# Attention block: the fourth head's scores behind six more value products, and an early load of the exponential's table

## The chip, the cores and the metric

The kernel runs on one core of a Trainium2 chip. The metric is the device time of one execution in microseconds (us). The kernel before takes 1063.34 us, the median of 3 runs (1062.45 to 1063.61).

The core's engines each work through an instruction list of their own, in order, and wait for one another through semaphores: TensorE (PE in the profile, with its weight loads as PEld), VectorE (DVE), ScalarE (ACT), GpSimd (POOL), and SyncE (SP), which here only starts DMA transfers.

## The reference, cut to what matters

The model has two layers. Each layer is a gated feed-forward block, a mixer (convolution, gated recurrence, pooling), cross attention to a memory of 256 rows, and a second feed-forward block, each followed by a layer norm. There are 256 tokens and the model width is 1024. The change is in the cross attention alone:

```python
def cross_attn(x, mem, wq, wk, wv, wo):
    bsz, s, _ = x.shape
    m = mem.shape[1]
    q = (x @ wq).reshape(bsz, s, CA_HEADS, CA_HEAD_DIM)
    k = (mem @ wk).reshape(bsz, m, CA_HEADS, CA_HEAD_DIM)
    v = (mem @ wv).reshape(bsz, m, CA_HEADS, CA_HEAD_DIM)
    sc = jnp.einsum('bshd,bmhd->bhsm', q, k).astype(jnp.float32) * (CA_HEAD_DIM ** -0.5)
    p = jax.nn.softmax(sc, axis=-1).astype(v.dtype)
    o = jnp.einsum('bhsm,bmhd->bshd', p, v).reshape(bsz, s, D_MODEL)
    return o @ wo
```

There are 4 heads of width 256. Everything is computed in float32.

## The kernel before, in words

Every matrix product is made of three products of halves. A float32 operand x is split into a high part (x rounded, one ScalarE copy, line 75) and a low part (x minus the high part, one VectorE subtraction, line 76), and a product is high x high, high x low and low x high, added up in PSUM. The helper `split` issues both steps, and the helper `product` (line 132) issues every one of these matrix products, so that most rows of TensorE have line 132 and most rows of ScalarE and VectorE have lines 75 and 76. Rows are told apart by their tiles.

A weight matrix comes in pieces of 512 KB into tiles named `raw` (6 buffers); ScalarE makes `whi` from each and VectorE `wlo` (8 buffers each). All loads of weights are started by SP.

The attention of one layer goes as follows. Heads are numbered from 0.

1. `values(l, 0, ...)`: values of heads 0 and 1 (columns 0 to 511), before the stretch that matters.
2. `query(0)`: the first 512 columns of the queries (heads 0 and 1), in two passes `p` of two column blocks each. A pass ends with `split(qTh, qTl, o)`: the queries' high part on ScalarE and their low part on VectorE.
3. `query(1, ...)`: the second 512 columns (heads 2 and 3). Between its two passes `weights(0)`, `deal(0)`, `weights(1)`, `deal(1)` are issued. Its first pass ends in the queries of head 2, its second in those of head 3.
4. `values(l, 1, ...)`: values of heads 2 and 3. Its loop runs over two blocks `i` of memory rows and 8 blocks `k` of the contraction, with three products for each; a dictionary says what is issued in front of a pair of blocks. Key 2 is i = 0, k = 4; key 3 is i = 0, k = 6; keys 6 and 7 are i = 1, k = 4 and k = 6. Before, key 2 holds `weights(2)`, `weights(3)`, then `turned(0)`, `turned(1)`, `deal(2)`, `deal(3)`.
5. `project_back`: the output projection, whose slabs of two contraction blocks need `xT`, the attention's output; between the first slab and the rest it issues `others`, that is `turned(2)`, `turned(3)`, `mixed(2)` and `mixed(3)`.

`weights(hh)` is a head's 12 score products into a PSUM tile `dn`, a row maximum (line 1372) and its scaling (line 1373) on VectorE, two exponentials on ScalarE (line 1379, tile `e`), and the reciprocal and scaling on VectorE (lines 1384 and 1387). `deal(hh)` is four transfers of 64 KB from `e` to `dealt`, started by SP (line 1395). `turned(hh)` transposes blocks on VectorE (line 1404) and splits the result into `pTh` and `pTl`, or, for heads 2 and 3, into the places of `qTh` and `qTl`. `mixed(hh)` is 12 products of those with the values and the split of their sums into `xTh` and `xTl`.

ScalarE reads its functions from a table. The compiler puts an ACT_TABLE_LOAD in front of an activation whose function is not in the table that is loaded; in the attention this is the exponential of head 0.

The order on each engine is set when the program is built, by a scheduler that follows the order in which the code issues instructions and lets an engine take a later instruction first where its own estimate has it ready earlier. `tc.issue_after(x)` ties an instruction behind x on x's engine.

Of the kernel before, what the change touches and what calls it, by code (L numbers as in the profile page):

```python
# [8 lines left out]
F32 = mybir.dt.float32  # L9
F32R = mybir.dt.float32r  # L10
U8 = mybir.dt.uint8
AF = mybir.ActivationFunctionType
# [5 lines left out]
P = 128  # L18
# [42 lines left out]
def model(ctx: ExitStack, tc: tile.TileContext, t: dict, out: bass.AP):  # L61
    nc = tc.nc
    cst = ctx.enter_context(tc.tile_pool(name="cst", bufs=1))
    wp = ctx.enter_context(tc.tile_pool(name="wp", bufs=1))
    sm = ctx.enter_context(tc.tile_pool(name="sm", bufs=2))
    ps = ctx.enter_context(tc.tile_pool(name="ps", bufs=4, space=PSUM))

    def acc(shape=(P, 2, SEQ), tag="acc"):
        return ps.tile(list(shape), F32, tag=tag, name=tag)
# [4 lines left out]
    def split(hi, lo, src):  # L74
        rounded = nc.scalar.copy(hi, src)  # L75
        lows.append(nc.vector.tensor_tensor(lo, src, hi.bitcast(F32), op=ALU.subtract))  # L76
        return rounded
# [63 lines left out]
    def mm_cols(w, cols, x):  # L141
        o = acc()
        for k in range(NK - 1):
            product(o, w.at(k, cols)[0], x[:, k], k == 0, False)
        for k in range(NK):
            product(o[:, 0, :], w.at(k, cols)[1], x[:, k, 0, :], False, False)
        product(o, w.at(NK - 1, cols)[0], x[:, NK - 1], False, True)
        return sums(o)

    def add(dst, o):  # L150
        dst = dst if len(dst.shape) == 3 else halves(dst)
        nc.scalar.copy(dst, o[:, 1])
        nc.vector.tensor_tensor(dst, o[:, 0], dst, op=ALU.add)  # L153


    def mm_rows(o, xh, xl, wh, wl, start, stop, more=False):
        product(o, xh, wh, start, False, more)
        product(o, xh, wl, False, False, more)
        product(o, xl, wh, False, stop, more)

    def tok(i):
        return slice(i * P, (i + 1) * P)
# [7 lines left out]
    nhalf = cst.tile([P, 16], F32, name="nhalf")[:, 0:HEADS]  # L170
# [151 lines left out]
    def ln_params(l, n):  # L322
        g = wp.tile([P, DM], F32, tag="lng", name="lng")
        b = wp.tile([P, DM], F32, tag="lnb", name="lnb")
        nc.sync.dma_start(g, t["ln_g"][l, n : n + 1, :].to_broadcast([P, DM]))
        nc.sync.dma_start(b, t["ln_b"][l, n : n + 1, :].to_broadcast([P, DM]))
        return g, b
# [645 lines left out]
    def values(l, c, vh, vl, between={}, held=None):  # L973
        w = load(t["ca_v"][l], 0, NK, c * CHUNK, CHUNK, across=True)
        for i in range(NT):
            o = acc((P, 512))
            for k in range(NK):
                if k % 2 == 0:
                    between.get(4 * i + k // 2, lambda: None)()
                wh, wl = w.at(k, slice(0, CHUNK))  # L980
                mm_rows(o, mT[:, k, 0, tok(i)], mT[:, k, 1, tok(i)], wh, wl, k == 0, k == NK - 1)
            d = slice(c * CHUNK, (c + 1) * CHUNK)
            part = (halves(vh[:, i, d]), halves(vl[:, i, d]), sums(o))
            if held is None or i:
                split(*part)
            else:
                nc.scalar.copy(part[0], part[2])
                held.append(part)
# [352 lines left out]
    def attention(l, pend):  # L1341
        scale = (DM // HEADS) ** -0.5
        with tc.tile_pool(name="att", bufs=1, reuse_waits="tile") as ap:
            qTh = ap.tile([P, NK, SEQ], F32R, name="qTh")
            qTl = ap.tile([P, NK, SEQ], F32R, name="qTl")
# [4 lines left out]
            def query(c, between=None):  # L1350

                with tc.issue_after(normed[-1].ins):
                    w = load(t["ca_q"][l], 0, NK, c * CHUNK, CHUNK, across=True)
                for p in range(2):
                    o = sm.tile([P, 2, SEQ], F32, tag="sums", name="sums", bufs=1)
                    for j in range(2):
                        add(o[:, j, :], mm_cols(w, slice((2 * p + j) * P, (2 * p + j + 1) * P), xT))
                    d = slice(4 * c + 2 * p, 4 * c + 2 * p + 2)
                    split(qTh[:, d, :], qTl[:, d, :], o)
                    if between is not None and p == 0:  # L1360
                        between()

            def weights(hh):
                o = acc(tag="dn")
                for i in range(NT):
                    for d in (2 * hh, 2 * hh + 1):
                        mm_rows(
                            o[:, i, :], qTh[:, d, tok(i)], qTl[:, d, tok(i)], kTh[:, d, :], kTl[:, d, :],
                            d == 2 * hh, d != 2 * hh,
                        )  # L1370
                mx = sm.tile([P, NT], F32, tag="mx", name="mx")
                nc.vector.tensor_reduce(mx, o, axis=AX.X, op=ALU.max)
                nc.vector.tensor_scalar_mul(mx, mx, -scale)


                e = ap.tile([P, NT * SEQ], F32, tag="e", name="e", bufs=2)
                s = sm.tile([P, NT], F32, tag="sum", name="sum")
                for i in range(NT):
                    nc.scalar.activation(  # L1379
                        e.rearrange("p (a m i j) -> p i m a j", m=2, i=2, j=32)[:, i],  # L1380
                        o[:, i, :].rearrange("p (a j h) -> p h a j", h=2, j=32),
                        AF.Exp, bias=mx[:, i : i + 1], scale=scale, accum_out=s[:, i : i + 1],
                    )
                nc.vector.reciprocal(s, s)
                for i in range(NT):
                    v = e.rearrange("p (q i j) -> p i q j", i=2, j=32)[:, i]
                    nc.vector.tensor_scalar_mul(v, v, s[:, i : i + 1])
                es[hh] = e


            def deal(hh):
                e = es[hh]
                x = ap.tile([P, 4, 4, 32], F32, tag="dealt", name="dealt", bufs=2)
                for a in range(4):
                    nc.sync.dma_start(x[a * 32 : a * 32 + 32], e[:, a * P : (a + 1) * P])
                pr[hh] = x

            def turned(hh):

                if hh < 3:  # L1400
                    pt = sm.tile([P, 2, SEQ], F32, tag="sums", name="square", bufs=1)
                else:
                    pt = ap.tile([P, NT * SEQ], F32, tag="e", name="e", bufs=2).rearrange("p (m t) -> p m t", m=2)
                nc.vector.transpose(pt.rearrange("p m (i b r) -> p b (m i) r", i=2, b=4), pr[hh])
                if hh < 2:
                    pTh = ap.tile([P, NT, SEQ], F32R, tag="pTh", name="pTh", bufs=2)
                    pTl = ap.tile([P, NT, SEQ], F32R, tag="pTl", name="pTl", bufs=2)
                else:

                    pTh, pTl = (x[:, 2 * hh - 4 : 2 * hh - 2, :] for x in (qTh, qTl))  # L1410
                split(pTh, pTl, pt)
                return pTh, pTl
# [19 lines left out]
            pT = []  # L1432
            held = []

            def turned_rows():
                pend()
                hi, lo, o = held.pop()
                with tc.issue_after(lows[-1].ins):
                    lows.append(nc.vector.tensor_tensor(lo, o, hi.bitcast(F32), op=ALU.subtract))

            values(l, 0, vh, vl, {6: turned_rows}, held)
            query(0)
            gb = ln_params(l, 2)
            query(1, lambda: (weights(0), deal(0), weights(1), deal(1)))
            values(
                l, 1, vh, vl,
                {
                    2: lambda: (weights(2), weights(3), pT.extend((turned(0), turned(1))), deal(2), deal(3)),

                    6: lambda: mixed(0, pT[0]),  # L1450
                    7: lambda: mixed(1, pT[1]),
# [18 lines left out]
    for l in range(DEPTH):  # L1470
        started, pend = ffn(
            l, "ffn1", 0, pend, early=None if l else beginnings, started=started,
            following=(lambda: key_weights(l, 0, True)) if l else None,
        )
        keys(l, 0, {6: pend}, started)
        pend = mixer(l, lambda: keys(l, 1))
        pend = attention(l, pend)
        end = l == DEPTH - 1
        started, pend = ffn(
            l, "ffn2", 3, pend, last=end,  # L1480
            following=None if end else lambda: load(t["ffn1_gate"][l + 1], 0, NK, 0, CHUNK, hold=True),
        )
# [27 lines left out]
```

## Time and profile before

| | |
|---|---|
| median of 3 runs | 1063.34 us |
| the profiled execution's own time | 1062.75 us |
| its span, first to last instruction | 1061.0 us |
| TensorE busy | 1050.8 us, 99% of the span |
| VectorE busy | 921.5 us, 87% |
| ScalarE busy | 667.4 us, 63% |
| mean granted TensorE clock | 0.998 |
| TensorE's share of the chain that ended last | 96% |

The profile is of one execution. Times in the prediction are microseconds from the start of its span. A row of the timeline has a start, a duration, the engine, the line, the operation, the tiles (out <- in), the shape, and how many equal instructions it merges; in brackets stands the engine's idle time ahead of it and what ended it. Matmuls overlap, so a row's duration is longer than the step from its start to the next start; the step is what a product costs. The chain that ended last is followed back from the last instruction: at each step to what released it, or to the instruction ahead of it on its engine.

The attention's stretch that the change touches lies at 313 to 348 us in layer 0 and at 836 to 871 us in layer 1.

### The profile page before, as it was taken

Reading aid. Unit: us, or ns where it says so; the run is one execution under the profiler, and the core shown is the slowest. Engines: PE = TensorE matmul, PEld = TensorE weight load, DVE = VectorE, ACT = ScalarE, POOL = GpSimd, SP = SyncE. Lnnn points to the kernel's source line nnn. Section 1 sums busy time; section 2 is a strip of 40 time slices with the busy share of each in tenths; the row PEclk is TensorE's granted clock in tenths of the full one; section 3 lists DMA queues with packets and bytes.
Section 4 is the critical chain, followed back from the end, with each engine's and each line's share of the span. In section 5 each row is a group of like instructions: output and inputs, shape, how many; then the busy total and the mean of one; then the engine's idle time right before and its main releaser. Section 6 shows DMA issues by size and latency. Waiting matters only on the chain.

```text
span 1061.0 us, 16440 instructions
## 1 busy us (share of the span) xinstructions
PE 1050.8 (99%) x5998; PEld 933.0 (88%) x5998; DVE 921.5 (87%) x1228; ACT 667.4 (63%) x917; POOL 99.6 (9%) x137
## 2 busy tenths in 40 slices
PE   9999999999999999999999999999999999999997
PEld 7888888889898888888888888998998998888896
DVE  6998898989898789887898887899898888888787
ACT  6675775676657567655665656666775655675661
POOL 8002001000100001010001001010001000000001
PEclk9999999999999999999999999999999999999999
DMA  9999984854775589978789988876637775799972
GB/s 362 297 300 298 260 276 145 268 166 155 231 252 197 168 281 233 365 187 229 230 302 258 339 220 217 269 229 222 204 119 231 250 235 169 244 297 297 236 199 69
DMA packets 142689, 252.11 MB, mean 238 GB/s; under 512 B 11376, under 2 KB 52112, under 8 KB 142608
## 3 DMA queue, kind: packets, MB, share of 16 engines
q1 hardware_dynamic: 130656, 228.89, 65.2%
q0 software_dynamic: 11376, 20.99, 11.4%
q10 hardware_dynamic: 576, 1.18, 0.3%
q8 instruction: 47, 0.77, 0.3%
q14 instruction: 34, 0.28, 0.1%
HBM read 234.50 MB, written 1.05 MB: 222 GB/s over the span
## 4 chain that ended last, share of the span: by engine, by line
PE 96%; DVE 2%; ACT 1%; DMA 1%; issue 0%; DVEq 0%; ACTq 0%; SPq 0%
PE acc L132 62%; PE dn L132 30%; DVE wlo L76 1%; PE acc L203 1%; PE dn L1174 0%; DMA raw<-in_ca_v_dram 0%; ACT whi L75 0%; PE dn L1248 0%; DMA h<-in_x_dram 0%; ACT e L1379 0%; DVE qTl L76 0%; PE acc L615 0%; PE dn L1247 0%; PE dn L1236 0%; DVE sums L153 0%
## 5 line engine op out<-in xcount | busy, mean ns | idle before, releaser
L76 DVE TENSOR_TENSOR wlo<-raw,whi 128x1024 fp32r<-128x1024 f32 (+1 forms) x452 | 533.5, 1211 | 58.5 <-ACT whi L75 51.9
L75 ACT CAST whi<-raw 128x1024 fp32r<-128x1024 f32 (+1 forms) x452 | 456.4, 1041 | 184.9 <-PE acc L132 48.7
L132 PE MATMUL acc<-whi,xT 128*128 128x512 f32 (+1 forms) x1064 | 313.9, 372 | 0.0
L132 PEld LDWEIGHTS acc<-whi,xT 128*128 128x128 f32 x1064 | 199.1, 189 | 26.9 <-DVE halves L755 0.3
L132 PE MATMUL acc<-wlo,xT 128*128 128x512 f32 (+1 forms) x532 | 197.9, 372 | 0.0
L132 PE MATMUL dn<-whi,ah 128*128 128x512 f32 x346 | 131.5, 380 | 0.0
L132 PE MATMUL dn<-wlo,ah 128*128 128x512 f32 x346 | 131.2, 379 | 0.0
L132 PE MATMUL dn<-whi,al 128*128 128x512 f32 x346 | 131.1, 379 | 0.0
L132 PE MATMUL acc<-xT,whi 128*128 128x512 f32 x480 | 118.6, 381 | 0.0
L132 PEld LDWEIGHTS acc<-wlo,xT 128*128 128x128 f32 x532 | 100.6, 189 | 13.4
L132 PEld LDWEIGHTS acc<-xT,whi 128*128 128x128 f32 x480 | 86.5, 190 | 9.5
L132 PE MATMUL dn<-whi,xT 128*128 128x512 f32 x288 | 87.4, 380 | 0.0
L132 PEld LDWEIGHTS dn<-whi,al 128*128 128x128 f32 x346 | 65.4, 189 | 9.2
L132 PEld LDWEIGHTS dn<-wlo,ah 128*128 128x128 f32 x346 | 65.4, 189 | 9.2 <-DVE wlo L76 0.3
L132 PEld LDWEIGHTS dn<-whi,ah 128*128 128x128 f32 x346 | 65.4, 189 | 8.9
L132 PEld LDWEIGHTS acc<-xT,wlo 128*128 128x128 f32 x480 | 63.8, 191 | 3.8
L132 PE MATMUL acc<-xT,wlo 128*128 128x256 f32 x480 | 64.5, 275 | 0.0
L132 PE MATMUL acc<-whi,kTh 128*128 128x512 f32 (+1 forms) x176 | 62.0, 352 | 0.0
L132 PE MATMUL acc<-wlo,kTh 128*128 128x512 f32 (+1 forms) x176 | 61.7, 351 | 0.0
L132 PE MATMUL acc<-whi,kTl 128*128 128x512 f32 (+1 forms) x176 | 61.7, 351 | 0.0
L132 PEld LDWEIGHTS dn<-whi,xT 128*128 128x128 f32 x288 | 54.4, 189 | 7.7 <-DVE xT L76 0.3
L132 PE MATMUL dn<-wlo,xT 128*128 128x512 f32 x144 | 54.6, 379 | 0.0
(261 smaller groups left out, 1287.6 us busy)
## 6 DMA issues: line engine op xcount, KB each, us to landing
raw<-in_ffn_up_dram SPq DMA_DIRECT2D x88, 512.0 KB, 5.8
raw<-in_ffn_down_dram SPq DMA_DIRECT2D x88, 512.0 KB, 6.0
raw<-in_ffn_gate_dram SPq DMA_DIRECT2D x84, 512.0 KB, 5.5
raw<-in_w_in_dram SPq DMA_DIRECT2D x48, 512.0 KB, 4.7
dealt<-sg SPq DMA_DIRECT2D x80, 128.0 KB, 4.8
raw<-in_ffn_up_dram POOLq DMA_DIRECT2D x19, 512.0 KB, 6.3
raw<-in_ffn_gate_dram POOLq DMA_DIRECT2D x16, 512.0 KB, 9.2
raw<-in_ca_k_dram SPq DMA_DIRECT2D x16, 512.0 KB, 5.0
```

The source lines that it names most:

```text
L75: rounded = nc.scalar.copy(hi, src)
L76: lows.append(nc.vector.tensor_tensor(lo, src, hi.bitcast(F32), op=ALU.subtract))
L132: turns.append(nc.tensor.matmul(o, w, x, start=start, stop=stop, skip_group_check=more))
L203: turns.append(nc.tensor.transpose(pt[:, k - 4 * j, :], of_k, unit))
```

## The change

Two things are changed, both in the attention of each layer.

- `weights(3)` and `deal(3)` are moved from key 2 to key 3 of `values(l, 1, ...)`: the six products of k = 4 and 5 now stand between the scores of head 2 and those of head 3, and `turned(0)`, `turned(1)` and `deal(2)` are issued ahead of head 3.
- Behind the last high part of `query(0)` ScalarE gets one activation of 128x1 elements, the exponential of a constant, into a tile `ready` that nothing reads. The tile takes a turn in the two buffers named `rs`. The table load is therefore placed there, and no longer in front of head 0's exponential.

```diff
                     d = slice(4 * c + 2 * p, 4 * c + 2 * p + 2)
-                    split(qTh[:, d, :], qTl[:, d, :], o)
+                    rounded = split(qTh[:, d, :], qTl[:, d, :], o)
                     if between is not None and p == 0:
                         between()
+                return rounded
...
             values(l, 0, vh, vl, {6: turned_rows}, held)
-            query(0)
+            rounded = query(0)
+            with tc.issue_after(rounded.ins):
+                nc.scalar.activation(sm.tile([P, 1], F32, tag="rs", name="ready"), nhalf[:, 0:1], AF.Exp)
             gb = ln_params(l, 2)
             query(1, lambda: (weights(0), deal(0), weights(1), deal(1)))
             values(
                 l, 1, vh, vl,
                 {
-                    2: lambda: (weights(2), weights(3), pT.extend((turned(0), turned(1))), deal(2), deal(3)),
+                    2: lambda: (weights(2), pT.extend((turned(0), turned(1))), deal(2)),
+                    3: lambda: (weights(3), deal(3)),
```

The built programs differ in the attention of the two layers and nowhere else, in the same way in both. Lines behind the added ones are one to four higher in the changed kernel.

On TensorE, where the scores of heads 2 and 3 stand in the middle of the value products (`dn` is a head's scores, `acc` the sum of the values):

```order
 L132 MATMUL dn<-kTl,qTh 128x256
 L132 MATMUL dn<-kTh,qTl 128x256
+L132 MATMUL acc<-whi,mT_1456 128x512
+L132 MATMUL acc<-wlo,mT_1456 128x512
+L132 MATMUL acc<-whi,mT_1456 128x512 x2
+L132 MATMUL acc<-wlo,mT_1456 128x512
+L132 MATMUL acc<-whi,mT_1456 128x512
 L132 MATMUL dn<-kTh,qTh 128x256
 L132 MATMUL dn<-kTl,qTh 128x256
```

Six value products moved from behind head 3's scores to a place between head 2's and head 3's.

On ScalarE, from the end of the first query chunk to where head 0's exponential follows:

```order
 L75 CAST whi<-raw 128x1024
 L75 CAST qTh<-sums 128x512
+L1445 ACT_TABLE_LOAD
+L1445 ACTIVATE ready<-nhalf 128x1
 L152 COPY sums<-acc 128x256 x2
 L75 CAST qTh<-sums 128x512
-L1379 ACT_TABLE_LOAD
```

The table load moved ahead of three copies and casts of the second chunk's first pass, with the small activation behind it.

On VectorE, behind the value products of i = 0, from the low parts of two weight pieces (`wlo`) on; `xT` is the attention's output, the transpose is head 2's; first as it was:

```order
L76 TENSOR_TENSOR wlo<-raw,whi 128x1024 x2
L76 TENSOR_TENSOR xT<-acc,xT 128x256
L1404 STREAM_TRANSPOSE square<-dealt 128x4x4x32
L76 TENSOR_TENSOR xT<-acc,xT 128x256
L76 TENSOR_TENSOR wlo<-raw,whi 128x1024
L76 TENSOR_TENSOR xT<-acc,xT 128x256
```

and as it is now:

```order
L76 TENSOR_TENSOR wlo<-raw,whi 128x1024 x2
L76 TENSOR_TENSOR xT<-acc,xT 128x256
L1405 STREAM_TRANSPOSE square<-dealt 128x4x4x32
L76 TENSOR_TENSOR wlo<-raw,whi 128x1024
L76 TENSOR_TENSOR xT<-acc,xT 128x256 x2
L76 TENSOR_TENSOR qTl<-square,qTh 128x512
```

The low part of one weight piece moved ahead of the second low part of head 0's output (`xT`).

On SP, the transfers behind the dealing of heads 0 and 1 (`raw` from `ca_o` are pieces of the output projection, from `ffn_gate` and `ffn_up` of the next block's weights):

```order
 L103 DMA raw<-in_ca_o_dram 128x1024 x2
-L103 DMA raw<-in_ffn_gate_dram 128x2x512
-L1395 DMA dealt<-e 32x4x128 x8
-L103 DMA raw<-in_ffn_gate_dram 128x2x512 x3
+L103 DMA raw<-in_ffn_gate_dram 128x2x512 x2
+L1396 DMA dealt<-e 32x4x128 x8
+L103 DMA raw<-in_ffn_gate_dram 128x2x512 x2
 L103 DMA raw<-in_ffn_up_dram 128x2x512 x4
```

A second piece of the next block's gate weights moved ahead of the eight transfers that deal heads 2 and 3.

## The prediction

> **What bounds the kernel now.** I read the page first, then who waited for whom on TensorE, then the chain that ended last through the attention, and last the timelines of the engines in it.
>
> ```profile
> span 1061.0 us, 16440 instructions
> PE 1050.8 (99%) x5998; PEld 933.0 (88%) x5998; DVE 921.5 (87%) x1228; ACT 667.4 (63%) x917; POOL 99.6 (9%) x137
> PE dn L596 <- DVE kTh L591: 1.5, 1, 1.5
> PE dn L132 <- DVE qTl L76: 0.6, 2, 0.4
> PE acc L615 <- DMA h<-in_x_dram: 0.4, 1, 0.4
> ```
>
> TensorE is the bound. Its waits are three rows. The first and third are the program's start; the middle one, twice, is for `qTl`, the low part of the queries. So an edit in the attention can win what hangs on that row, or nothing. The chain through layer 0's attention shows where it comes from:
>
> ```profile
> 315.51 2.68 PE dn L132 x24
> 318.19 2.64 PE acc L132 x16
> ...
> 321.84 0.66 ACT e L1379 x3
> ...
> 327.49 0.70 DVE qTl L76
> ...
> 328.23 1.38 PE dn L132 x10
> 329.61 10.45 PE acc L132 x60
> ```
>
> From 320.83 to 328.23 the chain leaves TensorE: over exponentials and what stands behind them to `qTl` of head 3, for which head 3's scores wait. Then TensorE again. The starts of the products tell what the wait costs (heads 0 and 1 first, then layer 0's heads 2 and 3, then layer 1's):
>
> ```profile
> 315.35 0.27 PE L132 MATMUL dn<-kTh,qTh 128*128 128x256 f32 x1
> 318.03 1.68 PE L132 MATMUL acc<-xT,whi 128*128 128x512 f32 x7
> ...
> 323.27 0.38 PE L132 MATMUL acc<-whi,mT 128*128 128x512 f32 x1
> 325.86 0.27 PE L132 MATMUL dn<-kTh,qTh 128*128 128x256 f32 x1
> 327.38 0.38 PE L132 MATMUL dn<-kTh,qTh 128*128 128x256 f32 x1
> 328.23 0.38 PE L132 MATMUL dn<-kTh,qTl 128*128 128x256 f32 x1 [0.35 <-DVE qTl L76]
> 329.44 0.38 PE L132 MATMUL acc<-whi,mT 128*128 128x512 f32 x1
> ...
> 849.14 0.27 PE L132 MATMUL dn<-kTh,qTh 128*128 128x256 f32 x1
> 851.07 0.38 PE L132 MATMUL dn<-kTh,qTl 128*128 128x256 f32 x1 [0.20 <-DVE qTl L76]
> 852.28 0.38 PE L132 MATMUL acc<-whi,mT 128*128 128x512 f32 x1
> ```
>
> Heads 0 and 1 put 24 score products into 318.03 - 315.35 = 2.68 us, 0.112 each, with no wait. The same 24 for heads 2 and 3 take 329.44 - 325.86 = 3.58 us in layer 0 and 852.28 - 849.14 = 3.14 us in layer 1. The stall is 0.90 + 0.46 = **1.36 us**, more than the bracketed idle time, since the starts behind a wait are also spread.
>
> **The change part by part.**
>
> *Six products ahead of head 3.* Nothing is added. Twelve value products take 325.86 - 323.27 = 2.59 us, so six take 1.30. Head 2 starts at 325.86 as before and its 12 products end at 327.20; the six end at 328.50; head 3's third product, the first to read `qTl`, comes two steps later, at 328.72. `qTl` was there at 327.49 + 0.70 = 328.19, so this edit alone covers it, by 0.5 us. In layer 1 the need moves to 849.14 + 1.34 + 1.30 + 0.22 = 852.00, and 851.07, when the waiting product started, bounds the readiness: 0.9 us. The high part is cast ahead of the low part and is covered with it.
>
> *The table load in front of the second chunk.*
>
> ```profile
> 313.19 0.61 ACT L75 CAST qTh<-sums 128x512 fp32r<-128x512 f32 x1
> 315.75 0.65 ACT L152 COPY sums<-acc 128x256 f32<-128x256 f32 x2 [1.94 <-DVE qTl L76]
> ...
> 319.27 1.28 ACT L1379 ACT_TABLE_LOAD   x1 [1.16 <-DVE mx L1373]
> 320.56 0.47 ACT L1379 ACTIVATE e<-dn,mx 128x256 f32<-128x256 f32 x1
> 320.94 0.19 ACT L1379 ACTIVATION_READ_ACCUMULATOR e<-dn,mx 128x1 f32 x1
> ...
> 838.86 0.65 ACT L152 COPY sums<-acc 128x256 f32<-128x256 f32 x2 [1.95 <-PE acc L132]
> 842.11 1.28 ACT L1379 ACT_TABLE_LOAD   x1 [0.88 <-DVE mx L1373]
> ```
>
> The load, 1.28 us, leaves the path of the exponentials and lands in a gap of 1.94 us (1.95 in layer 1) between a cast and the copies. With it goes one activation of 128x1, which the trace does not have. From below it is bounded by the 128x1 read of the accumulator, 0.19, from above by an exponential over 256 columns, 0.47; I take 0.2, as its size is that of the first. So 1.47 to 1.75 us in a gap of 1.94: cost nothing, hidden by ScalarE's wait for the copies' inputs. Without that cover, each 0.1 us over delays the copies, whose queries head 2 reads at 325.86, ten microseconds later: still nothing on TensorE, only less of the gain for the exponentials. The gain is up to 1.28 us on all that stands behind them on ScalarE: copy, casts, `qTh` of head 3, and so `qTl`, to 328.19 - 1.28 = 326.9. That alone would meet the old need at 327.20 + 0.22 = 327.42. Both edits remove the same stall, each alone; they do not add. The second one adds margin, not time.
>
> *What is late next.* TensorE comes 0.90 us earlier to all that follows, and head 3's scores end at 328.50 + 1.34 = 329.84 against 329.44, 0.40 us later. The rows that carry what follows:
>
> ```profile
> 333.51 0.62 DVE L1387 TENSOR_SCALAR e<-e,sum 128x256 f32<-128x256 f32 x2
> 335.25 2.35 DVE L76 TENSOR_TENSOR wlo<-raw,whi 128x1024 fp32r<-128x1024 f32 x2
> 337.85 0.71 DVE L1404 STREAM_TRANSPOSE square<-dealt 128x512 f32<-128x512 f32 x1
> 338.47 0.39 DVE L76 TENSOR_TENSOR xT<-acc,xT 128x256 fp32r<-128x256 f32 x1
> 339.32 1.23 DVE L76 TENSOR_TENSOR wlo<-raw,whi 128x1024 fp32r<-128x1024 f32 x1 [0.46 <-ACT whi L75]
> 341.62 0.59 PE L132 MATMUL dn<-whi,xT 128*128 128x512 f32 x2
> 344.05 0.68 DVE L76 TENSOR_TENSOR qTl<-e,qTh 128x512 fp32r<-128x512 f32 x1
> 346.42 0.28 PE L132 MATMUL acc<-qTh,vh 128*128 128x256 f32 x1
> ```
>
> Head 3's scaling ended at 334.13; I put it at 334.5 to 334.7. The two low parts behind it started at 335.25 because `pTl` and `vl` stood between; in the new order these come earlier, so the pair starts at about 334.7, 0.55 earlier. The second `xT` low part ended at 338.86. Now one low part of a weight (1.23) is ahead of it: 338.86 - 0.55 + 1.23 = 339.5. The first slab's product that reads it started at 341.62 and would now at 340.72. The slack falls from 2.8 to **1.2 us**, and stays positive. For head 3's `qTl<-e`, 344.73 before, the same items stand ahead in another order; I put it between 344.1 and 344.7. Its reader, one step after 346.42 - 0.90, comes at 345.6: about 0.9 to 1.5 us. Nothing is lost.
>
> *The transfers.*
>
> ```profile
> 333.47 5.08 SPq L1395 DMA_DIRECT2D dealt<-e  x8
> dealt<-e SPq DMA_DIRECT2D x32, 64.0 KB, 2.1
> dealt<-both SPq DMA_DIRECT2D x6, 64.0 KB, 4.8
> raw<-in_ffn_gate_dram SPq DMA_DIRECT2D x84, 512.0 KB, 5.5
> ```
>
> A second gate piece of 512 KB now starts ahead of the dealing of heads 2 and 3. It needs a `raw` buffer that VectorE frees with the weight's low part behind `qTl` (328.19 + 1.23 = 329.4 before, up to 1.28 earlier now), so it does not hold SP, which has nothing else to start until head 2 is scaled. Head 2's scaling should end near 332.7 and its four transfers, 0.63 us apart, start by 334.6 and land 2.1 us later, 336.7, ahead of the transposition, wanted at 337.85 - 0.55 = 337.3. The gate piece, at 5.5 us, started near 328.2, lands at 333.7, before most of them start. I take 2.1.
>
> The Trainium skill (DMA: Bandwidth & Descriptors, "Queues, rings and completion order") says that on each DMA engine the descriptors of one issuing queue are consumed in ring order, so that the dealing would wait for what is left of the gate piece. The two rows of `dealt` spread from 2.1 to 4.8, which fits, but nothing here shows that the ring is why. By that rule the sum would lose up to what the second rival below gives; by the row of 2.1 it loses nothing.
>
> **The sum.** The profiled execution took 1062.75 us, 1.75 around its span of 1061.0. Less 1.36 that is 1061.39. The median of the runs stands 0.59 above the profiled time: 1061.39 + 0.59 = **1062.0 us**, 0.13% faster. That is inside the 0.2% (2.1 us) that a measurement of this kernel can tell from no change.
>
> **The rivals.**
>
> *First: ScalarE's path is the bound, and the whole table load is won.* The chain passes through the exponentials in both layers, which speaks for it: 2 x 1.28 = 2.57 us, 1062.75 - 2.57 + 0.59 = 1060.8 us. Against it, the three rows of waits: TensorE waits for nothing else there, and work that comes earlier than TensorE needs it is worth nothing.
>
> *Second, slower: the dealing lands late behind the added gate piece.* The transposition then stands at the head of VectorE's queue, and the weight's low part and the second `xT` low part wait behind it. At 4.8 us, as for `dealt<-both`, head 2's last transfer lands at 339.4, 2.1 after it is wanted; past the slack of 1.2 that is 0.9 us in each layer: 1.8 - 1.36 = +0.4, or 1063.8 us. It costs from a landing time of 3.9 us on, and turns the sign at 4.6; at 5.5, as for the gate pieces themselves, it would be 1.6 per layer, 3.2 - 1.36 = +1.8, and 1065.2 us. Against it, the gate piece should have landed before. The rule of ring order raises its chance from 2 to 5 in 100.
>
> *Third: the wait moves and the time stays.* The first slab (slack 1.2) or head 3's mixing (0.9 to 1.5) waits instead, because my placing of VectorE's work may be a microsecond off. The price is at most what was won: 1062.75 to 1061.39, plus 0.59, so 1062.0 to 1063.3; I call it 1063.0.
>
> *Fourth: the change does not do what it says.* The built order has both moves, and the load waits for nothing ahead of it; only the small activation could hold ScalarE. At 0.47 it still fits. I give it 1 in 100, at 1063.3.
>
> **How the numbers follow.** Forecast 0.75, first rival 0.09, second 0.05, third 0.10, fourth 0.01. The three runs lie 0.89 below to 0.27 above their median. The range goes from the first rival's 1060.8, with a little of that spread, to the third's 1063.3 and the second's 1063.8: **1060.6 to 1063.8 us**. Faster by over 0.2% (below 1061.2): the first rival and about a tenth of the forecast's runs, 0.16. Slower by over 0.2% (above 1065.5): the second rival beyond a landing of 5.7 us and stray runs, 0.04. Within: 0.80.
>
> **What would show it.** TensorE's waits should lose the `qTl` row in both layers. From head 2's first product to the next value product behind head 3 there should be 2.68 + 1.30 = 3.98 us. ScalarE should show a load of 1.28 and an activation of about 0.2 behind `qTh`, with the copies starting at the same distance from it as before, and the first exponential right behind `mx`, about 1.3 us earlier. Transfers of `dealt` should land in 2.1 us. The forecast is wrong if the span shrinks by more than 2 us (first rival), if VectorE idles ahead of its transposition of `dealt` (second), or if TensorE gets a row of waits for `xT` or for the transposed weights (third).

## The result, and the profile after

The changed kernel takes 1061.46 us, the median of 22 executions, against 1063.55 us for the kernel before in 22 executions on the same chip: a ratio of 0.9981, 95% interval 0.9975 to 0.9987, so 2.0 us less (the medians themselves differ by 2.1). The forecast was 1062.0 us, 1.36 us less. With all later executions pooled (44 of the changed kernel, 155 of the kernel before, on several chips) the means differ by 2.0 us, with an interval of 1.7 to 2.3 from resampling them. So the direction was forecast and the size was too small; most of what follows is about that difference.

The page of the changed kernel, and its table of what TensorE waited for:

```profile
span 1061.0 us, 16436 instructions
PE 1050.1 (99%) x5998; PEld 932.8 (88%) x5998; DVE 920.5 (87%) x1228; ACT 668.8 (63%) x919; POOL 99.8 (9%) x137
PE dn L596 <- DVE kTh L591: 1.5, 1, 1.5
PE acc L132 <- DVE halves L755: 1.5, 2, 1.3
PE acc L615 <- DMA h<-in_x_dram: 0.4, 1, 0.4
```

The row for `qTl` is gone. The span is no shorter than that of before, because this one execution (1062.78 us, 1.3 above the median) has two waits, 1.5 us together, for `halves` in the feed-forward blocks (1.3 of it in layer 1's second one), which the profile of before does not have. One profile against one profile would have read as no change; the attention has to be looked at by itself. The timeline of TensorE there, layer 0, heads 2 and 3:

```profile
326.31 0.27 PE L132 MATMUL dn<-kTh,qTh 128*128 128x256 f32 x1
...
328.94 0.27 PE L132 MATMUL dn<-kTh,qTh 128*128 128x256 f32 x1
...
329.17 0.28 PE L132 MATMUL dn<-kTh,qTl 128*128 128x256 f32 x1
...
330.28 0.38 PE L132 MATMUL acc<-whi,mT 128*128 128x512 f32 x1
```

From head 2's first product to the value product behind head 3 it takes 330.28 - 326.31 = 3.97 us (forecast 3.98): 24 score products, six value products, no wait. ScalarE around the load, and VectorE's low part of head 3's queries:

```profile
313.41 0.61 ACT L75 CAST qTh<-sums 128x512 fp32r<-128x512 f32 x1
314.04 1.28 ACT L1445 ACT_TABLE_LOAD   x1
315.33 0.20 ACT L1445 ACTIVATE ready<-nhalf 128x1 f32<-128x1 f32 x1
315.96 0.65 ACT L152 COPY sums<-acc 128x256 f32<-128x256 f32 x2 [0.42 <-DVE qTl L76]
...
319.21 0.47 ACT L1380 ACTIVATE e<-dn,mx 128x256 f32<-128x256 f32 x1 [0.90 <-DVE mx L1374]
```

```profile
326.84 0.68 DVE L76 TENSOR_TENSOR qTl<-sums,qTh 128x512 fp32r<-128x512 f32 x1
```

Load and activation take 1.28 + 0.20 us and leave 0.42 of the gap. The low part is there at 327.52, and its reader starts at 329.17.

### The profile page after: what moved, and what is told of

Its sections match the earlier page's. It is cut to its first block, busy times and chain, and to the rows that moved or that the text cites. A ratio compares the mean times of both kernels' runs of the same rounds, so it can differ in the third digit from the quotient of the medians.

```text
span 1061.0 us, 16436 instructions
## 1 busy us (share of the span) xinstructions
PE 1050.1 (99%) x5998; PEld 932.8 (88%) x5998; DVE 920.5 (87%) x1228; ACT 668.8 (63%) x919; POOL 99.8 (9%) x137
## 4 chain that ended last, share of the span: by engine, by line
PE 89%; DMA 4%; DVE 3%; issue 2%; ACT 1%; POOL 0%; SPq 0%; DVEq 0%; ACTq 0%; POOLq 0%
PE acc L132 59%; PE dn L132 27%; DMA raw<-in_ffn_gate_dram 2%; DVE wlo L76 2%; DMA raw<-in_ffn_up_dram 1%; PE acc L203 1%; ACT whi L75 1%; DMA raw<-in_ffn_down_dram 1%; PE dn L1174 0%; PE dn L1248 0%; DVE raw L736 0%; PE dn L1247 0%; PE dn L1236 0%; PE acc L1316 0%; POOL raw L772 0%
```

## The experiments

Two lengths are used below. The **stretch** of the attention goes from TensorE's first product of line 203 ahead of it to the first of line 203 behind it; the **stall** is the time from head 2's first product to the value product behind head 3, less 2.68 us for the 24 score products, and less the value products that lie between the heads (1.30 for six, 3.89 for 18). Here are the two rows that bound the stretch in layer 1 of the third profile of the kernel before, 885.10 - 820.45 = 64.65 us:

```profile
820.45 1.05 PE L203 MATMUL acc<-udn,h 128*128 128x128 f32 x8
...
885.10 1.04 PE L203 MATMUL acc<-pdn,h 128*128 128x128 f32 x8
```

All profiles together (us; layer 0, layer 1):

| kernel | stretch | stall |
|---|---|---|
| before | 64.25, 63.82 | 0.90, 0.46 |
| before, second profile | 64.41, 63.77 | 1.07, 0.42 |
| before, third profile | 64.29, 64.65 | 0.94, 1.30 |
| before, 13 products added | 65.00, 64.87 | 0.75, 0.96 |
| before, one cast twice | 63.65, 63.75 | 0.30, 0.40 |
| changed, three profiles | 63.34 to 63.35 in both layers | none |
| six products alone; load alone | 63.34 to 63.35 in both layers | none |
| changed, three loads | 63.35, 63.35 | none |
| changed, 13 products added | 64.24, 63.90 | none |
| old order, three loads | 63.59, 63.72 | 0.25, 0.36 |
| changed, head 3 twelve products later | 63.70, 63.70 | none; 0.35 and 0.35 further on |

### Each part alone, and both kernels again

My theory: both edits remove the same stall, so each alone gives the whole. The rival: they add, or ScalarE's path is the bound and the load is won whole.

> The kernel before once more, unchanged, beside itself: a measure of what this comparison can tell, and a second profile of it. Stall theory (the 1.36 us of waiting for the queries' low part is all there is): ratio 1.000, and the same stall of 0.9 and 0.5 us between head 2's first product and the value product behind head 3. Rival (the kernel before mostly runs with another wait of some 0.7 us, which its first profile did not have, since that execution was among the fastest of the kernel): this profile shows a wait on TensorE that the first did not.

> The whole change again, on the same chip as its halves. Stall theory: the same time as each half within 0.3 us, ratio 0.9987. Rival (the edits add, and the whole is worth the 2.1 us that the medians showed): ratio 0.9981, clearly below both halves.

The kernel before again: 1064.55 us, ratio 1.0002 [0.9994, 1.0011]. Its second profile has the stall, 1.07 and 0.42 us, and also what the rival of that run looked for: TensorE waited 1.4 us for `halves` and 0.8 us for `sg` in feed-forward blocks, where the first profile has no such wait. That execution was the slowest of its 12 (1065.92 us). The changed one again: 1061.56 us, 0.9976 [0.9967, 0.9985].

The six products alone leave out the load:

```diff
-            rounded = query(0)
-            with tc.issue_after(rounded.ins):
-                nc.scalar.activation(sm.tile([P, 1], F32, tag="rs", name="ready"), nhalf[:, 0:1], AF.Exp)
+            query(0)
```

> Only the six products between heads 2 and 3; the table load stays in front of head 0's exponential. Stall theory: the stall is gone in both layers, 3.98 us from head 2's first product to the value product behind head 3, and the time falls by 1.4 us (ratio 0.9987), as with both edits. Rival (the two edits add, the load is worth up to 1.28 us in each layer): less than the whole change, ratio nearer to 0.9993, and a wait for qTl that stays.

Measured: 1062.02 us, 0.9982 [0.9973, 0.9991]. The low part and its first reader in layer 0 (VectorE, then TensorE):

```profile
327.61 0.68 DVE L76 TENSOR_TENSOR qTl<-sums,qTh 128x512 fp32r<-128x512 f32 x1
```

```profile
328.82 0.28 PE L132 MATMUL dn<-kTh,qTl 128*128 128x256 f32 x1
```

It ends at 328.29, 0.53 us before it is read; the forecast said 0.5.

The load alone leaves the products where they were:

```diff
-                    2: lambda: (weights(2), pT.extend((turned(0), turned(1))), deal(2)),
-                    3: lambda: (weights(3), deal(3)),
+                    2: lambda: (weights(2), weights(3), pT.extend((turned(0), turned(1))), deal(2), deal(3)),
```

> Only the table load in front of the second query chunk; heads 2 and 3 are scored back to back as before. Stall theory: qTl of head 3 comes up to 1.28 us earlier, to about 326.9 against a need of 327.4 in layer 0, so the stall is gone here too and the ratio is 0.9987. Casts that wait for a weight buffer can eat some of the 1.28; then a rest of the stall of up to 0.3 us stays. Rival (the edits add): 1.36 us less a part that is missing, ratio nearer to 0.9993.

Measured: 1061.75 us, 0.9980 [0.9972, 0.9989]. TensorE in layer 0, from head 2's first product to the value product behind head 3:

```profile
325.91 0.27 PE L132 MATMUL dn<-kTh,qTh 128*128 128x256 f32 x1
...
327.47 0.28 PE L132 MATMUL dn<-kTh,qTl 128*128 128x256 f32 x1
...
328.58 0.38 PE L132 MATMUL acc<-whi,mT 128*128 128x512 f32 x1
```

2.67 us, back to back. The two halves and the whole agree within their intervals and have the same stretch to 0.01 us: the edits do not add. If the load had been won whole, the load alone would have shortened each of the two stretches of before by 1.28; against the first profile it shortened them by 0.91 and 0.48, the stall there and no more.

### Three loads in the gap

This asks what lies behind the claim that a lost cover costs nothing, and what a load costs. In front of the second query chunk stand three switches of the table and not one:

```diff
-                nc.scalar.activation(sm.tile([P, 1], F32, tag="rs", name="ready"), nhalf[:, 0:1], AF.Exp)
+                for f in (AF.Exp, AF.Silu, AF.Exp):
+                    turn = nc.scalar.activation(sm.tile([P, 1], F32, tag="rs", name="ready"), nhalf[:, 0:1], f)
```

> The whole change, with two more switches of ScalarE's table behind the first in front of the second query chunk: three loads and three activations of 128x1 where the change has one of each (exponential, another function, exponential; nothing reads them). By the rows of the changed kernel a load and its activation are 1.28 + 0.20 us, so three are 4.4 us in a gap of 1.94: the copies of the second chunk start 2.5 us later. The prediction said that a lost cover costs nothing on TensorE with the six products in place. Its theory in numbers: head 0's first exponential has 0.90 us of idle time ahead of it and comes some 1.2 to 1.6 us later; head 3's queries come as much later, 328.7 to 329.1 against a need of 329.2 in layer 0: no stall, or a few tenths, time 1061.4 to 1062.2, head 2's first product to the value product behind head 3 still 3.97 us. Rival 1, each load also costs a drain of about 1.4 us that the rows do not show: the copies are 6 to 7 us late, and TensorE stalls 4 us or more in each layer. Rival 2, a bank or a weight that TensorE needs from ScalarE is late before the queries are: a new wait row in the second query chunk, 1 to 2 us in each layer.

Measured: 1061.65 us, 0.9978 [0.9969, 0.9986]: nothing lost. ScalarE in layer 0:

```profile
314.03 1.28 ACT L1446 ACT_TABLE_LOAD   x1
315.32 0.20 ACT L1446 ACTIVATE ready<-nhalf 128x1 f32<-128x1 f32 x1
315.54 1.28 ACT L1446 ACT_TABLE_LOAD   x1
316.84 0.20 ACT L1446 ACTIVATE ready<-nhalf 128x1 f32<-128x1 f32 x1
317.06 1.28 ACT L1446 ACT_TABLE_LOAD   x1
318.35 0.20 ACT L1446 ACTIVATE ready<-nhalf 128x1 f32<-128x1 f32 x1
318.46 0.63 ACT L152 COPY sums<-acc 128x256 f32<-128x256 f32 x2
...
320.16 0.47 ACT L1380 ACTIVATE e<-dn,mx 128x256 f32<-128x256 f32 x1
```

From the first load to the copies are 318.46 - 314.03 = 4.43 us for three loads with their activations, 1.48 each on the mean. Counted from the start of the stretch (296.74 here, 296.90 in the changed kernel's profile), the copies come 2.7 us later, the first exponential 1.1, and head 3's low part 0.5 (31.11 against 30.62): ScalarE's own waits behind the copies, 0.90 us of them ahead of the first exponential in the changed kernel, took in most of the rest. The Trainium skill ("ScalarE: Activation LUTs", section "What ACT_TABLE_LOAD costs") adds a drain of about 1380 ns to a load of 1283 ns. The measured load, 1.28 us, agrees; the drain is not in these rows, where the next activation starts 0.01 to 0.02 us behind the end of each load and the copies 0.11 us behind the start of the last activation. By the Trainium skill's figures three switches would be about 8.0 us, an estimate.

The same three loads with head 3's scores back behind head 2's:

> As the run with three loads, but with the products in the order of the kernel before (head 3's scores right behind head 2's), that is the early load alone with two more switches. Without the six products head 3's low queries are needed 1.30 us earlier, at 327.9 in layer 0 of the changed kernel's clock. Prediction's theory (both edits act on the same wait, one by an earlier arrival, the other by a later need): the stall comes back, 0.8 to 1.2 us in each layer, 1.6 to 2.4 in all, and the time returns to 1063.2 to 1064.2; the row of waits for qTl is there again. Rival, ScalarE is not what sets the arrival of the queries: no stall, 1061.7 as with the early load alone. With a drain behind each load it would be 5 us or more in each layer.

Measured: 1062.27 us, 0.9989 [0.9980, 0.9997], 0.6 us above the three loads with the change's order. The two intervals overlap, so the rows decide and not the times: the stall is back, 0.25 and 0.36 us. TensorE in layer 0:

```profile
327.77 0.28 PE L132 MATMUL dn<-kTl,qTh 128*128 128x256 f32 x1
328.03 0.38 PE L132 MATMUL dn<-kTh,qTl 128*128 128x256 f32 x1
```

The step from 327.77 to 328.03 is 0.26 where 0.11 is the pace. The table of waits has no row for this, so the idle time in brackets is not the place to look for stalls of this size; the steps are. The mechanism held, the size did not: I had expected 0.8 to 1.2 in each layer, because I passed on to the queries more of ScalarE's lateness than got there.

### Head 3 twelve products later still

```diff
-                    3: lambda: (weights(3), deal(3)),
+                    5: lambda: (weights(3), deal(3)),
```

> The whole change, but head 3's scores twelve products later still (18 value products between heads 2 and 3 and not 6), so 2.59 us later on TensorE and for all that hangs on head 3. The prediction saw 0.9 to 1.5 us of slack between head 3's transposed weights and the products that read them: by that, 1.1 to 1.7 us are lost in each layer, 2.2 to 3.4 in all, 1063.7 to 1064.9, with a row of waits for the transposed weights. Rival, the slack was put too small, since the transfers and VectorE's queue have room that the rows of before did not show: in the changed kernel the low part ended at 344.12 and its first reader started at 346.07, 1.95 us, and the last transfer of head 3 landed about 1.5 us before its transposition; then 2.59 us later cost 0 to 0.6 in each layer, 1061.5 to 1062.7.

Measured: 1062.62 us, 0.9990 [0.9982, 0.9999], about 1 us above the changed kernel. The scores show no stall; it comes where the transposed weights of head 3 are read (VectorE and TensorE, layer 0):

```profile
347.54 0.68 DVE L76 TENSOR_TENSOR qTl<-e,qTh 128x512 fp32r<-128x512 f32 x1
```

```profile
347.82 0.38 PE L132 MATMUL dn<-whi,xT 128*128 128x512 f32 x1
348.28 0.38 PE L132 MATMUL acc<-qTl,vh 128*128 128x256 f32 x1
348.49 0.28 PE L132 MATMUL acc<-qTh,vl 128*128 128x256 f32 x1
```

348.28 - 347.82 is 0.46 where 0.22 is the pace, and 0.1 more follows: 0.35 us, the same in layer 1. The rival held: of 2.59 us only 0.35 reached TensorE, so the room there was more than 2 us, not the forecast's 0.9 to 1.5. It is the changed kernel's 1.95 us, and 0.22 for one product of the output projection (`dn<-whi,xT` above) that the built order of this run puts in front of the waiting one. So the place that the change chose was well clear of the next wait.

### Putting the time back

Thirteen products of 256 columns (8 in layer 0, 5 in layer 1, 0.111 us each, 1.44 together) stand in front of head 3's mixing, once with the change and once without:

```diff
                 o = acc()
+                for _ in range((8 if l == 0 else 5) if hh == 3 else 0):
+                    product(o[:, 0, :], vh[:, 0, hh * 256 : hh * 256 + P], pT[0][:, 0, :], True, True)
```

> The whole change, with 13 products added in front of the first product of head 3's mixing (8 in layer 0, 5 in layer 1), each with the shape of the ones behind it (256 columns, 0.111 us from start to start) and overwritten by them; the result stays the same, and every other engine keeps its order. They put back the 1.45 us that the change took out of the attention (43.44 to 42.54 us in layer 0, 43.01 to 42.54 in layer 1). Theory 1, the gain is the attention's time and the 0.6 us by which the medians moved beyond it (2.1 against 1.4 to 1.5) is of another origin: the attention takes 43.4 and 43.1 us again, and the time stands 1.45 us above the change's, near 1063.0, some 0.6 us below the kernel before. Theory 2, what follows the attention answers to when it starts, so that the 0.6 us belong to the earlier start: they go too, and the time is that of the kernel before, 1063.5 to 1063.9, ratio 1.000. Rival, the wait that was won is still open on another engine and the products fill it: no loss, 1061.5.

> The kernel before with the 13 added products in front of head 3's mixing (8 in layer 0, 5 in layer 1; overwritten by the real ones, the result stays the same): the price of 1.45 us of attention, measured at the old order. Theory 1, TensorE's time passes one for one to the end: 1.45 above the kernel before, ratio 1.0014, near 1065.2. Theory 2, what follows loses more when it starts later (as 2.1 us were won by 1.43 in the attention): 2.1 above, ratio 1.0020, near 1065.8. Rival, the old order has idle time behind head 3 that takes the products in: no loss.

With the change: 1063.07 us, 0.9997 [0.9988, 1.0005], and stretches 0.89 and 0.55 us longer than the changed kernel's. Without: 1065.65 us, 1.0019 [1.0010, 1.0029]. So the rivals fell: added time on TensorE passes to the end, and no idle time takes it in. Both medians lie 1.5 to 2.0 above their kernel; the intervals hold 1.44 and 2.1 alike, so these runs do not settle whether what follows the attention answers to its start. The profile of the padded old order gave something else: its stalls were 0.75 and 0.96, not 0.90 and 0.46.

### The stall is not one number

> The kernel before once more, unchanged, for the part of the gain that the attention doesn't hold: the medians moved by 2.1 us, the attention by 1.43. Outside the attention the profiles differ only in the two second feed-forward blocks (155.43 to 156.55 us in layer 0, 158.04 to 159.63 in layer 1, from the end of the attention's last products to the next stage), where TensorE sometimes waits for halves behind a transfer that adds into a tile, and in the start. Theory 1, these waits come by chance in either order: this profile shows any value of that range, as the changed ones do. Theory 2, the order of before has them more often or longer: both blocks above 155.6 and 158.2, as in the two profiles of it so far.

> The changed kernel once more, unchanged, beside the kernel before. Theory 1 (the rest of the gain is chance in the feed-forward): the ratio comes nearer to 0.9987, which is the attention's 1.43 us, and the second feed-forward blocks show any value of the range. Theory 2 (it belongs to the change): 0.9980 again, and the blocks at 155.4 and 158.0 to 158.2.

The kernel before: 1063.76 us, 1.0001 [0.9992, 1.0010]. The changed one: 1061.87 us, 0.9984 [0.9975, 0.9992]. The second theory of the first of these runs fell: the feed-forward blocks of before took 155.43 and 158.04 us, the lowest there are. The second run decides nothing: the changed kernel's blocks took 155.43 and 158.04 us too, and its interval holds both theories' ratios. The attention showed more. TensorE in layer 1 of the kernel before, third profile:

```profile
849.86 0.27 PE L132 MATMUL dn<-kTh,qTh 128*128 128x256 f32 x1
...
851.79 0.38 PE L132 MATMUL dn<-kTh,qTh 128*128 128x256 f32 x1 [0.43 <-ACT qTh L75]
...
852.62 0.38 PE L132 MATMUL dn<-kTh,qTl 128*128 128x256 f32 x1 [0.34 <-DVE qTl L76]
...
853.84 0.38 PE L132 MATMUL acc<-whi,mT 128*128 128x512 f32 x1
```

3.98 us where the first profile had 3.14: a stall of 1.30 and not 0.46. ScalarE tells why, in the same execution:

```profile
835.70 1.05 ACT L75 CAST whi<-raw 128x1024 fp32r<-128x1024 f32 x1 [0.69 <-DMA raw<-in_ca_v_dram]
...
837.86 0.62 ACT L75 CAST qTh<-sums 128x512 fp32r<-128x512 f32 x1
...
851.09 0.65 ACT L75 CAST qTh<-sums 128x512 fp32r<-128x512 f32 x1
```

ScalarE waited 0.69 us for a piece of the value weights to land. The copy behind its cast was late, VectorE's addition waited for that copy (1.12 us here, 0.20 in the first profile), and all that follows on both engines shifted by 0.84 us, from the cast at 837.86 (17.41 us into the stretch, against 16.57) to head 3's low part (32.11 against 31.28). In every profile of the old order, the stall is the low part's lateness past 30.97 us into the stretch, plus 0.15 (to within 0.02).

The third profile of the changed kernel had the same mishap in the same layer:

```profile
834.72 1.05 ACT L75 CAST whi<-raw 128x1024 fp32r<-128x1024 f32 x1 [0.50 <-DMA raw<-in_ca_v_dram]
...
836.88 0.62 ACT L75 CAST qTh<-sums 128x512 fp32r<-128x512 f32 x1
```

The cast starts 17.34 us into the stretch and the low part ends at 30.79, and yet the stretch is 63.34. So the change took out not a stall of 1.36 but one that differs from execution to execution.

The last run tried to make this lateness by hand, with the cast of the first chunk's last queries written twice in the kernel before:

```diff
+                    if c == 0 and p == 1:
+                        nc.scalar.copy(qTh[:, d, :], o)
                     split(qTh[:, d, :], qTl[:, d, :], o)
```

> The kernel before with one ScalarE cast written twice: the high part of the last queries of the first chunk, in front of the gap in which the change puts its load (the result stays the same, and no engine's order changes otherwise). It puts all that ScalarE and VectorE do for the second query chunk 0.5 to 0.6 us later, as a weight piece that lands late does by itself in the profiles: over eight layers' attention of the old order the stall of head 3's scores is the lateness of the queries' low part past 30.97 us from the attention's first product, plus 0.15 (low part at 31.23 to 32.11, stall 0.42 to 1.30). Theory, the stall follows whatever the casts start with: low part 0.5 to 0.6 later than it would be, stalls of 0.9 to 1.9 in each layer, two layers 2.6 to 3.1 in all against a mean of 1.70, the kernel 1.0 to 1.2 us slower than before: ratio 1.0010, near 1064.8. Rival, the late low parts are a by-product of something on TensorE or VectorE that is late in the same executions: the cast is taken in by the gap or the waits behind it, and stall and time stay, ratio 1.000.

Measured: 1063.72 us, 0.9997 [0.9988, 1.0006]: a miss. ScalarE in layer 0:

```profile
313.02 0.62 ACT L1360 CAST qTh<-sums 128x512 fp32r<-128x512 f32 x1
313.67 0.62 ACT L75 CAST qTh<-sums 128x512 fp32r<-128x512 f32 x1
315.76 0.65 ACT L152 COPY sums<-acc 128x256 f32<-128x256 f32 x2 [1.47 <-DVE qTl L76]
```

The gap shrank from 1.94 to 1.47 and the copies came no later (18.95 us into the stretch, against 19.29 in the first profile). They wait for the low part of those queries, which stands on VectorE behind two low parts of weights, and these do not wait for this cast. So the cast was put off the path. The run bears out that the gap belongs to VectorE's queue, but the step from a late piece to a long stall stays read from the rows of executions in which it happened, not made at will. This profile had no wait for value weights in either layer, and the smallest stalls of all, 0.30 and 0.40, which fits.

## Why the prediction was right, and where it was short

**What bounds the kernel, and what could be won: right.** The `qTl` row went in both layers, and with it the stall and nothing more. No new row stands in its place in the attention.

**Each edit alone covers it; they do not add: right**, by the runs with one part each. The worked margins of the six products, 0.5 and 0.9 us, were 0.53 and 0.9. The load alone brought the low part to 30.61 us into the stretch in both layers, 0.36 ahead of the old need. That the second edit adds margin and not time can be seen in the late executions: a low part at 32.11, as in the third profile of before, would leave the six products alone 0.16 us, and one at 30.79, as in that of the changed kernel, would leave the load alone 0.18, where both together had 1.48 (worked out from the old need at 30.97 and the six products' 1.30; neither part alone was run with a piece that late).

**The load costs nothing in the gap: right.** 1.28 and 0.20 were forecast and measured, and even three loads cost nothing with the six products in place. "Up to 1.28 us" was too much for the low part: it came 1.10 and 0.66 us earlier in the changed kernel, and never earlier than 30.60 into the stretch. The rows show where the rest went: the copy that follows the exponentials waits for TensorE's own products,

```profile
321.36 0.38 ACT L152 COPY sums<-acc 128x256 f32<-128x256 f32 x1 [0.21 <-PE acc L132]
```

and in none of the profiles with the early load does it start before 24.44 us into the stretch (25.92 and 25.49 in the first profile of before). No run moved those products.

**What is late next: right in sign and close in size.** The changed execution's clock is 0.45 us behind that of the forecast, as head 2 starts at 326.31. VectorE and TensorE in it:

```profile
334.44 0.62 DVE L1388 TENSOR_SCALAR e<-e,sum 128x256 f32<-128x256 f32 x2
335.17 2.36 DVE L76 TENSOR_TENSOR wlo<-raw,whi 128x1024 fp32r<-128x1024 f32 x2
...
339.51 0.74 DVE L76 TENSOR_TENSOR xT<-acc,xT 128x256 fp32r<-128x256 f32 x2
...
343.44 0.68 DVE L76 TENSOR_TENSOR qTl<-e,qTh 128x512 fp32r<-128x512 f32 x1
```

```profile
341.17 0.59 PE L132 MATMUL dn<-whi,xT 128*128 128x512 f32 x2
...
345.96 0.28 PE L132 MATMUL acc<-qTh,vh 128*128 128x256 f32 x1
```

Less 0.45, head 3's scaling ends at 334.6 (forecast 334.5 to 334.7) and the pair of low parts starts at 334.7 (forecast the same). The second `xT` low part is the first of the two at 339.51; it ends near 339.9, for a product at 341.17: 1.2 to 1.3 us of slack where 1.2 was worked out. Head 3's `qTl<-e` ends at 344.12 and is read one step behind 345.96, at 346.07: 1.95 us and not 0.9 to 1.5, so the third rival was further away than I put it.

**The second rival, late dealing, fell:**

```profile
dealt<-e SPq DMA_DIRECT2D x32, 64.0 KB, 2.1
```

2.1 us as before, with the second gate piece ahead of the dealing. The row is a median over all four heads and both layers; the eight transfers of heads 2 and 3 have 2.1 by themselves too, in either layer, and VectorE has no idle time ahead of their transpositions. The cost would have begun at 3.9.

**The first rival fell too**, although the median lies between its time and the forecast, and although the medians' 2.1 us is about what I had named as its sign, a span shorter by more than 2 us. That sign was too near the forecast to tell the two apart. What decides is the parts alone: by this rival the load alone should have taken 2.57 us out of the two stretches, and the six products none of that; both brought the stretches to the same 63.34 to 63.35.

**Where it was short: the size, 1.36 for 2.0.** The sum had one term for the gain, the stall "0.90 + 0.46 = 1.36", and I took the one profiled execution for the kernel. That execution ran 0.59 us below the median, and I added this back to the changed kernel as if it had nothing to do with the stall. The five profiles of the old order, two of them with an edit that leaves this order as it is, have stalls of 1.36, 1.49, 2.24, 1.71 and 0.70 in the two layers together: a mean of 1.50 with a scatter of 0.56, where the changed order has none. The three of the unedited kernel alone have a mean of 1.70. 1.50 is 0.14%, a ratio of 0.9986. The pooled gain is 2.0 [1.7, 2.3]; with five profiles the mean is good to about 0.25, so the 0.5 between them is not shown to be anything. The mean differs from the term by no more than its scatter allows, so the runs do not show that the stall is what was short. They show that its closeness was in part luck: a first profile like the last would have given 0.70, one like the third 2.24.

**What stays open** is whether part of that 0.5 lies in the second feed-forward blocks. TensorE there waits in some executions for `halves`, behind transfers that add into a tile. Over the lowest values seen (155.43 and 158.04 us) the five profiles of the old order spent 0 to 1.95 us, 0.80 on the mean, and the nine with the change or a part of it 0 to 1.59, 0.49 on the mean. The difference is smaller than the scatter. GpSimd starts the first of these that loads gate weights 51.4 us behind the end of the stretch in both orders (layer 0, first profiles), so the change does not move it against TensorE. One more block belongs here: layer 1's first feed-forward block took 155.43 us in all profiles of the old order but the second, where it took 156.48 with the wait for `sg`, and at most 155.58 in the nine. None of this is shown to belong to the change: it hangs on a few executions.

## What to carry to other kernels

A stall read off one execution is a sample: when what it waits for starts with a transfer's landing, profile the kernel several times before putting a number on it, and look for the late piece in each. Two edits that act on one wait, one by earlier arrival and one by later need, give one gain; choose by the margin that each leaves at the reader, which here was 0.5 us or more with the six products and 0.36 with the load. Measure stalls by the step from start to start: the idle time in brackets showed 0.35 of 0.90 us here, and nothing of the 0.25 and 0.36 that came back with three loads.

## What the runs showed of the hardware

- A switch of ScalarE's table cost what its row says: 1.28 us for the load, 0.20 for an activation of 128x1, 1.51 and 1.52 from one load to the next with three in a row.
- ScalarE's waits for the pieces of the value weights, 512 KB each, differ from execution to execution: none, 0.6 and 1.0 us in all in layer 1 of the three profiles of the changed kernel, with medians to landing of 5.1, 5.5 and 5.6 us. In the old order a wait of 0.69 us for one piece went with a longer stall on TensorE (1.30 us against 0.46).
- The transfers that add into a tile differ too, and TensorE's time goes with them. The rows of layer 1's second feed-forward block, first of the changed kernel's first profile, then of its third (the last number is the median time to landing):

```profile
raw<-in_ffn_gate_dram POOLq DMA_DIRECT2D x2, 512.0 KB, 11.6
```

```profile
raw<-in_ffn_gate_dram POOLq DMA_DIRECT2D x2, 512.0 KB, 9.8
```

At 11.6 us the block took 159.63 us, with a wait of 1.3 us for `halves` on TensorE; at 9.8 it took 158.04, with none.
